# Memory layer of a decoder step: where the low part of the next weights stands on VectorE around y_b

## The chip, the cores and the metric

The kernel runs on one core of a Trainium2 chip. The metric is the device time of one execution in microseconds (us); it is given as the median of several runs. The engines are TensorE (PE in the profile; PEld is its weight load), VectorE (DVE), ScalarE (ACT), GpSimd (POOL) and SyncE (SP), which here only issues DMAs.

## The reference

One inference step of a two-layer decoder trunk on 320 tokens: 256 tokens of a new sequence and 8 samples of 8 tokens, with a model width of 1024. Layer 0 mixes tokens with a gated MLP, layer 1 with an mLSTM matrix memory; each is followed by a gated MLP with a width-3 convolution. Everything is fp32. The part that matters here is the mixer of layer 1, the memory layer:

```python
def mlstm_mixer(x, ...):
    p = x @ w_in                       # q, k, v, o and two gates; 8 heads
    qk, new_buf = causal_dwconv(qk_pre, ...); qk = silu(qk)
    h, C, n, m = mlstm_chunkwise(q, k, v, ig, lf, C0, n0, m0)
    hn = (h - mu) * rsqrt(var + EPS) * gn_g
    y = (sigmoid(o_pre) * hn) @ w_out
    return y, new_buf, C, n, m
```

Per head the chunkwise memory computes `sc = q k^T` weighted by gates, `num = q C + sc v` with its denominator, and the new state `C = decay C + k^T v`.

## The kernel before

**Layout.** Activations lie transposed: 128 features on the partitions, 320 tokens (T) along the free axis. A weight matrix is cut into blocks of 128 outputs, each of 8 tiles of 128 x 128 (512 KB). fp32 products are made from two parts: `split` rounds a tensor to a high part (fp32r) and takes the rest as low part; a block of the memory layer is 8 tiles times (high x high, high x low) in one sweep and then 8 times low weights x high activations in a second sweep (`chunk` with `low_last`), 24 matmuls.

**Weights.** `take` hands out the next block. It first calls `prefetch` (L121), which keeps four raw blocks loaded ahead (`raw`, four buffers, DMAs on SP's queue, L127) and one block split ahead: the high part `wh` is a copy on ScalarE (L154), the low part `wl` a subtraction on VectorE (L155). `wh` and `wl` have three buffers each. A raw buffer is free for the next load when both parts are made.

**Order.** A scheduler places the instructions of each engine by their dependencies; only TensorE's matmuls and a few others keep the order of the program. `tc.issue_after(ins)` adds an edge that puts the following instructions behind `ins` on the engine of `ins`.

**The loop over heads** (`layer_b`, the loop with `for h in range(NH)`; "pass h" below). Pass h, for h = 1 to 6, takes six blocks of head h: q, k, two of v, two of o. Between them it finishes the head before it:
- `qk_epi` (L755 on) scales a block of q or k (`bpad`), convolves it on VectorE (`bcv`), applies tanh on ScalarE (`bth`), and makes `qs` and the parts `qh`, `qhl`, `kh`, `khl`.
- `inter` and `numer` accumulate `num` of head h-1 on TensorE; `stats` makes mean and variance (`ns`, `dn`, `bstat`, `mv`, `rd`, `t`, and a power on GpSimd, `sl`), `normed` the normalised `hn` on ScalarE.
- `state_sample(h-1, i)`, i = 0 to 3, makes the new states of two samples each: two matmuls `pcs`, two VectorE updates of `C` (L1007), one store `out_Cs` on SP.
- `scores(h)` multiplies q and k (`psc`, with `kh` and `khl`), and makes the gate weights `w` on ScalarE from a row broadcast, `Mb`, that `rows_in(h)` loads from memory on SP (L794).
- `o_epi` (L1011) scales a block of o (`o_b`, VectorE) and takes its tanh on ScalarE (`th_o`).
- `finish(h-1)` (L1018) transposes `hn` on TensorE into two PSUM tiles `phn`, multiplies each by `1 + th_o` of head h-1 on VectorE (`y_b`, L1027), and splits the result into `yhb` (ScalarE, L1029) and `ylb` (VectorE, L1030).
- `k_nat` and `v_nat` transpose k and v of head h (`pk`, `pv`) and make `kgs`, `kgh`, `kgl`, `vh`, `vl` of them; `state_split` makes the parts `Ch`, `Cl` of the old states.

PSUM is in two pools: `psm` (3 buffers) for the blocks, `pk` and half of `pcs`, and `psa` (5 buffers) for `num`, `psc`, `phn`, `pv`, the state of the prompt (`pCp`) and the other `pcs`. The buffer of the first `phn` goes to the next head's `num`.

From the end of pass 4 on, blocks of the output projection (`early`, the table `EARLY_OUT`) come between: two after pass 4's k and v, one and two in each of passes 5 and 6. Pass 7 is written out separately.

In `finish` each half e makes its transposes, its `y_b` and its two parts before the next half begins. The `wl` of the second block after the o blocks is asked for by a `take` that comes later in the program, but it depends on nothing made in between, and in passes 1 to 6 the scheduler puts it ahead of the second `o_b`.

Of the kernel before, what the change touches and what calls it, by code (L numbers as in the profile page):

```python
# [10 lines left out]
F32 = mybir.dt.float32  # L11
# [3 lines left out]
MULT, ADD, SUB, MAX = ALU.mult, ALU.add, ALU.subtract, ALU.max  # L15

P = 128
# [3 lines left out]
T = TP + NB * NS  # L21
# [16 lines left out]
class Net:  # L38
# [597 lines left out]
    def layer_b(self):  # L636
        nc, tc, I, O = self.nc, self.tc, self.I, self.O
# [4 lines left out]
        with ExitStack() as ctx:  # L642
# [143 lines left out]
            def v_epi(h, j, ps):  # L786
                vT = lp.tile([P, 384], F32, tag="vT", name="vTb", bufs=2)
                nc.scalar.copy(vT[:, :T], ps[:, :T])
                nc.scalar.copy(vT[:, T:384], ps[:, TP:T])
                S[h].setdefault("vT", []).append(vT)  # L790

            def rows_in(h):
                mb = hp.tile([P, 392], F32, tag="Mb", name="Mb", bufs=2)
                nc.sync.dma_start(mb, I["rows"][h:h + 1, :].to_broadcast([P, 392]))  # L794
                S[h]["rows"] = mb
# [110 lines left out]
            def state_split(h, i):  # L906
                C0 = S[h]["C"][i]
                Ch = lp.tile([P, 2, CW], F32R, tag="Ch", name="Ch", bufs=3)
                Cl = lp.tile([P, 2, CW], F32R, tag="Cl", name="Cl", bufs=3)
                nc.scalar.copy(Ch, C0)  # L910
                low = nc.vector.tensor_tensor(Cl, C0, Ch.bitcast(F32), op=SUB)  # L911
                S[h].setdefault("Cs", []).append((Ch, Cl))
                return low

            def inter(h, i):

                s = S[h]
                if i == 0:
                    s["num2"] = self.psa.tile([P, 512], F32, tag="pa", name="num")
                d = s["num2"][:, :CW]  # L920
                Ch, Cl = s["Cs"][i]
                for u in range(2):
                    b = 2 * i + u
                    lhs = Qz[:, b * P:(b + 1) * P]
                    mm(d, lhs, Ch[:, u, :], b == 0, False)
                    mm(d, lhs, Cl[:, u, :], False, False)

            def numer(h):
                s = S[h]
                Ph, Pl, dec = s["P"]  # L930
                num = [self.psa.tile([P, 512], F32, tag="pa", name="num") for _ in range(2)] + [s["num2"]]
                d = num[2][:, :CW]
                mm(d, Ps, vh[:, 2, :], False, True)
                d = num[0][:, :CW]
                mm3(d, Ph[:, 0:P], Pl[:, 0:P], vh[:, 0, :], vl[:, 0, :], True, True)
                d = num[1][:, :CW]
                mm3(d, Ph[:, P:TP], Pl[:, P:TP], vh[:, 0, :], vl[:, 0, :], True, False)
                mm3(d, Ph[:, TP:384], Pl[:, TP:384], vh[:, 1, :], vl[:, 1, :], False, True)
                s["num"] = num
# [44 lines left out]
            def state_prompt(h):  # L984
                s = S[h]
                kgh, kgl, _, _ = s["kg"]
                pc = self.psa.tile([P, 512], F32, tag="pa", name="pCp")
                for t in range(2):
                    mm3(pc[:, :CW], kgh[:, t, :], kgl[:, t, :], vh[:, t, :], vl[:, t, :], t == 0, t == 1)

                Cp = hp.tile([P, CW], F32, tag="Cp", name="Cp", bufs=1)
                nc.scalar.copy(Cp, pc[:, :CW])
                nc.sync.dma_start(O["Cp"][h], Cp)

            def state_sample(h, i):
                s = S[h]
                kgz, dec, C0 = s["kg"][3], s["P"][2], s["C"][i]

                wide = h < NH - 2
                pcs = [pool.tile([P, 512], F32, tag=tag, name="pcs") for pool, tag in  # L1000
                       ((self.psa, "pa"), (self.psm, "pm") if wide else (self.psa, "pa"))]
                for u in range(2):
                    b = 2 * i + u
                    mm(pcs[u][:, :CW], kgz[:, b, :], vh[:, 2, :] if b < 4 else vb, True, True)
                for u in range(2):
                    b = 2 * i + u
                    made = nc.vector.scalar_tensor_tensor(C0[:, u, :], C0[:, u, :], dec[:, b:b + 1], pcs[u][:, :CW], op0=MULT, op1=ADD)  # L1007
                nc.sync.dma_start(O["Cs"][h, :, 2 * i:2 * i + 2, :], C0)
                return made
# [5 lines left out]
                nc.scalar.activation(th, o, AF.Tanh, scale=0.5)  # L1015
                S[h].setdefault("o", []).append(th)

            def finish(h):  # L1018
                s = S[h]
                yh = hp.tile([P, 2, T], F32R, tag="yhb", name="yhb", bufs=6)  # L1020
                yl = hp.tile([P, 2, T], F32R, tag="ylb", name="ylb", bufs=6)
                for e in range(2):
                    pt = self.psa.tile([P, 512], F32, tag="pa", name="phn")
                    for t in range(3):
                        self.tr(pt[:, t * P:(t + 1) * P], hn[:, t, e * P:(e + 1) * P], self.ident)
                    y = self.tp.tile([P, T], F32, tag="yf", name="y_b", bufs=2)
                    nc.vector.scalar_tensor_tensor(y, s["o"][e], 1.0, pt[:, :T], op0=ADD, op1=MULT)  # L1027
                    g = gnh[:, 2 * h + e:2 * h + e + 1]
                    nc.scalar.activation(yh[:, e, :], y, AF.Copy, scale=g)  # L1029
                    nc.vector.scalar_tensor_tensor(yl[:, e, :], y, g, yh[:, e, :].bitcast(F32), op0=MULT, op1=SUB)  # L1030
                    Y[2 * h + e] = (yh[:, e, :], yl[:, e, :])

            def early(h, r):
                for m in self.EARLY_OUT.get((h, r), ()):
                    self.residual(m, self.block(8, lambda k: Y[k]))
# [25 lines left out]
            def blk():  # L1061
                return self.block(KD, self.x_rhs)
# [19 lines left out]
            for h in range(NH):  # L1082
                if h:
                    rows_in(h)
                    qk_epi(h, 0, blk())
                    early(h, 0)
                    if h == 1:
                        inter(0, 0)
                        state_split(0, 3)
                    inter(h - 1, 1)  # L1090
                    qk_epi(h, 1, blk())
                    for i in (2, 3):
                        inter(h - 1, i)
                    numer(h - 1)
                    early(h, 1)
                    ps = blk()
                    with self.behind_split():
                        stats(h - 1)
                    v_epi(h, 0, ps)
                    state_prompt(h - 1)  # L1100
                    made = state_sample(h - 1, 0)
                    early(h, 2)
                    v_epi(h, 1, blk())
                last = h == NH - 1
                if last:
                    with tc.issue_after(made.ins):
                        made = normed(h - 1)
                    states(h, made)
                if h:
                    made = state_sample(h - 1, 1)  # L1110
                    if not last:
                        with tc.issue_after(made.ins):
                            normed(h - 1)
                scores(h)
                early(h, 3)
                if h and not last:
                    o_epi(h, 0, blk())
                if last:
                    finish(h - 1)
                    begin(0)  # L1120
                if h:
                    for i in (2, 3) if last else (2,):
                        state_sample(h - 1, i)
                if last:
                    begin(1)

                    self.prefetch(0, self.used + 2)
                early(h, 4)
                if h and not last:
                    states(h, made)  # L1130
                if h and not last:
                    o_epi(h, 1, blk())
                if h and not last:
                    finish(h - 1)
                    state_sample(h - 1, 3)
                k_nat(h)
                v_nat(h)
                if h:
                    inter(h, 0)
                    for i in (2, 3):  # L1140
                        low = state_split(h, i)
                else:
                    with tc.issue_after(self.parts[0].ins), tc.issue_after(self.parts[1].ins):
                        state_split(0, 2)
                early(h, 5)
            nc.sync.dma_start(O["b_state"], nst)

            h = NH - 1
# [181 lines left out]
```

## Time and profile before

| | |
|---|---|
| median of 3 runs | 953.72 us (953.01 to 955.09) |
| the profiled execution | 954.62 us |
| its span, first to last instruction | 952.9 us |
| granted TensorE clock, mean | 0.999 |
| instructions | 17084 |
| read from and written to HBM | 143.05 MB and 11.99 MB, 163 GB/s over the span |
| `wl` on VectorE (L155), 256 of them | 298.8 us, 1.168 us each |
| `wh` on ScalarE (L154), 256 of them | 256.7 us, 1.004 us each |

The profile is of one execution. A page gives busy times by engine and a chain of waits, followed back from the last instruction; further views give groups by line and tile, the waits, busy time by stretch, and a timeline. In a timeline a row is: start (us from the span's start), duration (us), engine, line, operation, out<-in, sizes, count, and in brackets how long the engine had been idle before and what ended that. Rows of SP are DMA issues, not the transfers. Matmuls overlap: a row shows some 0.31 us for one of 320 columns, and the next starts 0.15 us after it.

### The profile page before, as it was taken

To read this page: it belongs to the slowest core of one execution; us is meant where nothing else is said; L and a number is where in the kernel's file an instruction comes from. 1 tells how busy PE (TensorE), PEld (TensorE's weight loads), DVE (VectorE), ACT (ScalarE), POOL (GpSimd) and SP (SyncE) were. 2 spreads that over 40 slices of the span, in tenths; PEclk is the share of its full clock that TensorE was granted. 3 is DMA by queue.
4 is the path that set the end of the run, shared out by engine and by line. 5 is a ranking of instruction groups with operands and counts; after the bars stand their busy time and mean duration, and the time that the engine had idled before them with its cause. 6 is when DMAs were issued, how large, how long until landed. Compare 5 with 4: busy or idle time off the path is not lost.

```text
span 952.9 us, 17084 instructions
## 1 busy us (share of the span) xinstructions
PE 945.6 (99%) x6420; PEld 932.8 (98%) x6420; DVE 695.6 (73%) x1324; ACT 530.5 (56%) x978; POOL 117.6 (12%) x291
## 2 busy tenths in 40 slices
PE   9999999999999999999999999999999999999997
PEld 8889999999999999999999999999999999999997
DVE  6766976577777764559999998788888777775443
ACT  7557543454554443348877767666765544554342
POOL 3200000010000000014442312303001000000000
PEclk9999999999999999999999999999999999999999
DMA  8643346544444455565465756654474444445541
GB/s 272 209 153 133 130 134 190 175 140 150 153 156 147 141 159 156 146 215 176 155 201 185 219 174 207 198 183 133 132 250 144 156 148 145 151 150 152 145 138 56
DMA packets 55238, 156.15 MB, mean 164 GB/s; under 512 B 7492, under 2 KB 13132, under 8 KB 55156
## 3 DMA queue, kind: packets, MB, share of 16 engines
q1 hardware_dynamic: 55156, 155.06, 51.2%
q8 instruction: 51, 0.84, 0.3%
q14 instruction: 31, 0.25, 0.1%
HBM read 143.05 MB, written 11.99 MB: 163 GB/s over the span
## 4 chain that ended last, share of the span: by engine, by line
PE 93%; DVE 3%; ACT 1%; issue 1%; POOL 0%; DMA 0%; SPq 0%; POOLq 0%; ACTq 0%
PE pm L54 80%; PE pv_a L54 6%; PE num L54 2%; PE pmix L54 1%; PE pcs L54 1%; PE pCp L54 1%; PE phn L57 0%; PE psc L54 0%; DVE wl L155 0%; PE pv L57 0%; PE pc L54 0%; ACT wh L154 0%; PE pg L54 0%; DVE Cl L911 0%; DMA raw<-in_a_wv 0%
## 5 line engine op out<-in xcount | busy, mean ns | idle before, releaser
L154 ACT CAST wh<-raw 128x1024 fp32r<-128x1024 f32 (+3 forms) x256 | 256.7, 1004 | 270.8 <-PE pm L54 141.5
L155 DVE TENSOR_TENSOR wl<-raw,wh 128x1024 fp32r<-128x1024 f32 (+3 forms) x256 | 298.8, 1168 | 121.0 <-ACT wh L154 116.5
L54 PE MATMUL pm<-xh,wh 128*128 128x320 f32 x1216 | 372.2, 311 | 0.0
L54 PE MATMUL pm<-xl,wh 128*128 128x320 f32 x1216 | 370.3, 309 | 0.0
L54 PE MATMUL pm<-xh,wl 128*128 128x320 f32 x1216 | 321.2, 309 | 0.0
L54 PEld LDWEIGHTS pm<-xl,wh 128*128 128x128 f32 x1216 | 228.4, 188 | 0.2
L54 PEld LDWEIGHTS pm<-xh,wh 128*128 128x128 f32 x1216 | 228.3, 188 | 0.2
L54 PEld LDWEIGHTS pm<-xh,wl 128*128 128x128 f32 x1216 | 214.5, 188 | 0.0
L54 PE MATMUL pm<-yh_f,wh 128*128 128x320 f32 x352 | 108.8, 309 | 0.0
L54 PE MATMUL pm<-yl_f,wh 128*128 128x320 f32 x352 | 108.8, 309 | 0.0
L54 PE MATMUL pm<-yh_f,wl 128*128 128x320 f32 x352 | 108.8, 309 | 0.0
L54 PEld LDWEIGHTS pm<-yh_f,wh 128*128 128x128 f32 x352 | 66.1, 188 | 0.0
L54 PEld LDWEIGHTS pm<-yl_f,wh 128*128 128x128 f32 x352 | 66.1, 188 | 0.0
L54 PEld LDWEIGHTS pm<-yh_f,wl 128*128 128x128 f32 x352 | 66.1, 188 | 0.0
L532 DVE SCALAR_TENSOR_TENSOR fcv<-fpad,vecs,fcv 128x336 f32<-128x336 f32 x88 | 49.5, 565 | 2.1 <-ACT fcv L530 0.6
L54 PE MATMUL pm<-yh_a,wh 128*128 128x320 f32 x128 | 39.6, 310 | 0.0
L54 PE MATMUL pm<-yh_a,wl 128*128 128x320 f32 x128 | 39.5, 309 | 0.0
L54 PE MATMUL pm<-yl_a,wh 128*128 128x320 f32 x128 | 39.5, 309 | 0.0
L534 ACT ACTIVATE fgl<-fcv 128x256 f32<-128x256 f32 x44 | 18.3, 415 | 37.9 <-DVE fcv L532 37.8
L54 PE MATMUL pm<-yhb,wh 128*128 128x320 f32 x128 | 38.2, 311 | 0.0
L54 PE MATMUL pm<-ylb,wh 128*128 128x320 f32 x128 | 37.9, 309 | 0.0
L304 DVE TENSOR_TENSOR xT<-pm,xT 128x320 f32<-128x320 f32 x39 | 19.0, 488 | 24.7 <-PE pm L54 24.5
(289 smaller groups left out, 1366.5 us busy)
## 6 DMA issues: line engine op xcount, KB each, us to landing
raw<-in_f_up SPq DMA_DIRECT2D x88, 512.0 KB, 3.3
raw<-in_b_win SPq DMA_DIRECT2D x48, 512.0 KB, 4.1
raw<-in_f_dn SPq DMA_DIRECT2D x32, 448.0 KB, 3.4
C<-in_C SPq DMA_DIRECT2D x32, 258.0 KB, 3.9
out_Cs<-C SPq DMA_DIRECT2D x32, 258.0 KB, 4.0
raw<-in_a_win SPq DMA_DIRECT2D x16, 512.0 KB, 3.2
raw<-in_a_wo SPq DMA_DIRECT2D x16, 512.0 KB, 4.0
raw<-in_f_dn SPq DMA_DIRECT2D x16, 512.0 KB, 3.6
```

The costliest lines, as they stand in the source:

```text
L54: self.pin(self.nc.tensor.matmul(out, lhsT, rhs, start=start, stop=stop, skip_group_check=skip))
L154: self.last_split = self.hold(nc.scalar.copy(wh[:, :kn, :], raw[:, :kn, :]))
L155: self.last_low = nc.vector.tensor_tensor(wl[:, :kn, :], raw[:, :kn, :], wh[:, :kn, :].bitcast(F32), op=SUB)
L304: self.nc.vector.tensor_tensor(x, ps[:, :T], x, op=ADD)
L532: nc.vector.scalar_tensor_tensor(cv, pd[:, i:i + NC], self.vec(w + i * KF), cv, op0=MULT, op1=ADD)
L534: nc.scalar.activation(gl[:, :TP], cv[:, :TP], AF.Gelu_apprx_tanh)
```

## The change

`finish` gets an argument. Both halves now make their transposes and their `y_b` first. In passes 1 to 6 the argument is true: then `prefetch` is called behind the second `y_b`, with the number of blocks to be split raised by one, so that one more block is split there and the next `take` finds it done; its `wl` has to stand behind the second `y_b` on VectorE. Then both halves make their two parts. The calls of `finish` in pass 7 and after the loop keep their order of work apart from both `y_b` standing before the parts.

```diff
-            def finish(h):
+            def finish(h, ahead=False):
                 s = S[h]
                 yh = hp.tile([P, 2, T], F32R, tag="yhb", name="yhb", bufs=6)
                 yl = hp.tile([P, 2, T], F32R, tag="ylb", name="ylb", bufs=6)
+                ys = []
                 for e in range(2):
                     pt = self.psa.tile([P, 512], F32, tag="pa", name="phn")
                     for t in range(3):
                         self.tr(pt[:, t * P:(t + 1) * P], hn[:, t, e * P:(e + 1) * P], self.ident)
-                    y = self.tp.tile([P, T], F32, tag="yf", name="y_b", bufs=2)
-                    nc.vector.scalar_tensor_tensor(y, s["o"][e], 1.0, pt[:, :T], op0=ADD, op1=MULT)
+                    ys.append(self.tp.tile([P, T], F32, tag="yf", name="y_b", bufs=2))
+                    made = nc.vector.scalar_tensor_tensor(ys[e], s["o"][e], 1.0, pt[:, :T], op0=ADD, op1=MULT)
+                if ahead:
+                    with tc.issue_after(made.ins):
+                        self.prefetch(0, self.used + 2)
+                for e, y in enumerate(ys):
                     g = gnh[:, 2 * h + e:2 * h + e + 1]
                     nc.scalar.activation(yh[:, e, :], y, AF.Copy, scale=g)
                     nc.vector.scalar_tensor_tensor(yl[:, e, :], y, g, yh[:, e, :].bitcast(F32), op0=MULT, op1=SUB)
...
-                    finish(h - 1)
+                    finish(h - 1, True)
```

## The prediction

> **What bounds the kernel now.** I read the page's busy times first, then busy time by stretch, then the waits of TensorE's weight loads.
>
> ```profile
> PE 945.6 (99%) x6420; PEld 932.8 (98%) x6420; DVE 695.6 (73%) x1324; ACT 530.5 (56%) x978; POOL 117.6 (12%) x291
> PE 93%; DVE 3%; ACT 1%; issue 1%; POOL 0%; DMA 0%; SPq 0%; POOLq 0%; ACTq 0%
> ```
> ```profile
> 450.00:480.00 30.00, 29.60 (x213) 29.14 (x212) 28.87 (x73) 25.56 (x65) 12.80 (x22) 1.00 0.48 157
> ```
> ```profile
> 480.00:720.00 240.00, 239.96 (x1723) 239.65 (x1722) 209.27 (x479) 165.94 (x364) 51.37 (x79) 1.00 0.59 186
> ```
> ```profile
> PEld num L54 <- DVE y_b L1027: 0.5, 1, 0.5
> ```
>
> The columns of a stretch are its length and the busy time of PE, PEld, DVE, ACT and POOL. TensorE bounds the kernel: it is 99% busy and carries 93% of the chain, at full granted clock. In the rest of the memory layer (480 to 720 us) it is idle for 0.04 us, so nothing on VectorE can save time there. From 450 to 480 us it is idle for 0.40 us, and VectorE works 28.87 of 30 us. The one wait on VectorE in this layer that is worth naming is that on y_b: once, 0.5 us. This is pass 1 of the loop over heads:
>
> ```profile
> 475.94 1.21 DVE L155 TENSOR_TENSOR wl<-raw,wh 128x1024 fp32r<-128x1024 f32 x1
> ```
> ```profile
> 476.92 0.82 PE L57 MATMUL pv<-ident,vTb 128*128 128x128 f32 x6
> 477.07 0.47 DVE L1013 TENSOR_TENSOR o_b<-pm,rb 128x320 f32<-128x320 f32 x1
> ```
> ```profile
> 477.47 0.87 DVE L1027 SCALAR_TENSOR_TENSOR y_b<-th_o,phn 128x320 f32<-128x320 f32 x2
> ```
> ```profile
> 477.99 0.39 PE L54 MATMUL num<-Ch,Qz 128*128 128x258 f32 x1 [0.26 <-DVE y_b L1027]
> ```
>
> The accumulator `num` takes the PSUM buffer that the first y_b empties, so y_b behind wl makes TensorE wait. The chain of waits, one pass later, has the same six transposes and `num` right behind them without a wait (columns: start, us, what):
>
> ```profile
> 505.93 0.66 PE pv L57 x6
> 506.58 0.47 PE num L54 x4
> ```
>
> So in pass 1 `num` could have started at 476.92 + 0.66 = 477.58; it started at 477.99.
>
> **The change, part by part.**
>
> *Removed at pass 1.* Without wl ahead, o_b starts at 475.94, the first y_b at 476.34 and is done by about 476.8, well ahead of 477.58. The gain is 0.41 us; its bounds are 0.26 (PE's own idle time in the last row) and the 0.50 of PEld. wl itself then runs from 477.13 to 478.26. It belongs to the second block ahead, which starts at 482.73 (next fence) and uses its low part last, so its own delay is covered by 4 us.
>
> ```profile
> 482.73 3.52 PE pm L54 x24
> ```
> ```profile
> 488.40 3.52 PE pm L54 x24
> ```
> ```profile
> 563.75 10.56 PE pm L54 x72
> ```
>
> *The same move in passes 2 to 6.* No wait on y_b is there to take away. wl was filler while VectorE waited for the block of o:
>
> ```profile
> 503.00 1.21 DVE L155 TENSOR_TENSOR wl<-raw,wh 128x1024 fp32r<-128x1024 f32 x1
> 504.81 0.49 DVE L1013 TENSOR_TENSOR o_b<-pm,rb 128x320 f32<-128x320 f32 x1 [0.60 <-PE phn L57]
> ```
>
> Now that gap stays partly empty and wl stands in front of y's low parts, the last state update (C), kgs, vl and the next head's work: all of it comes up to 1.13 us (475.94 to 477.07) later. No instruction and no transfer is added: there are as many wl, wh and raw loads as before. But the schedule follows. In the changed program's instruction order three things differ in passes 2 to 4:
> 1. On VectorE `ns` and a statistic stand ahead of q's and k's `qs`, and wl of the o block stands ahead of k's `qs`.
> 2. On ScalarE `ns`, `vh` and two `dn` stand ahead of `bth` (they were behind it).
> 3. On SP the order before the load of the next rows (Mb) was: out_Cs, raw, C, out_Cs, Mb. It is now: out_Cs, C, raw, out_Cs, Mb. raw waits for the moved wl, the second out_Cs for the moved C, and Mb queues behind both.
>
> The step that can hold TensorE is the last one, through Mb. In pass 3:
>
> ```profile
> 505.23 0.38 SPq L127 DMA_DIRECT2D raw<-in_b_win  x1
> 508.00 0.33 SPq L903 DMA_DIRECT2D C<-in_C  x1
> 508.42 0.39 SPq L1008 DMA_DIRECT2D out_Cs<-C  x1
> 508.86 0.42 SPq L794 DMA_DIRECT2D Mb<-rows  x1
> ```
> ```profile
> 514.42 1.04 ACT L811 ACTIVATE w<-Mb,cols 128x256 f32<-128x256 f32 x3 [1.53 <-DMA Mb<-rows]
> 515.37 1.04 ACT L154 CAST wh<-raw 128x1024 fp32r<-128x1024 f32 x1
> 516.31 1.14 ACT L910 CAST Ch<-C 128x516 fp32r<-128x516 f32 x2
> 517.35 0.49 ACT L772 ACTIVATE bth<-bcv 128x344 f32<-128x344 f32 x1
> 517.75 0.66 ACT L768 ACTIVATE bcv<-bpad,vecs 128x344 f32<-128x344 f32 x1
> 518.43 0.37 ACT L945 COPY ns<-num 64x258 f32<-64x258 f32 x1
> 518.83 0.41 ACT L861 CAST vh<-vh 32x256 fp32r<-32x256 f32 x1
> ```
> ```profile
> 506.41 1.18 DVE L1030 SCALAR_TENSOR_TENSOR ylb<-y_b,gnh,yhb 128x320 fp32r<-128x320 f32 x2
> ```
> ```profile
> 507.50 0.48 DVE L1007 SCALAR_TENSOR_TENSOR C<-C,Mb,pcs 128x258 f32<-128x258 f32 x1
> ```
> ```profile
> 522.96 0.26 DVE L312 TENSOR_TENSOR khl<-qs,kh 128x128 fp32r<-128x128 f32 x1
> ```
> ```profile
> 525.04 0.28 PE L54 MATMUL psc<-qh,khl 128*128 128x256 f32 x1
> ```
>
> ScalarE waits for Mb already now, with everything behind it, and TensorE needs khl at 525.04, 1.8 us after it is made. The working; on VectorE the next instruction starts 0.08 us ahead of the end that a row shows (wl: 1.21 shown, 1.13 to the next start), so each takes that much less than its row:
> - PE is 0.41 us early, so o_b starts at 504.40; o_b and both y_b take 1.18, wl 1.13, y's low parts 1.10, the two C 0.80: C is done at 508.6 (now 507.98). out_Cs follows at once, Mb 0.44 later: 509.05. It landed 5.56 us after issue here (508.86 to 514.42). So w starts at 514.6.
> - bth now stands behind w, wh, Ch (2.93 us), ns, vh (0.83) and two dn (0.2): it starts at w + 3.96 and ends at w + 4.4. Behind it on VectorE come qs, the three bcv of k (waiting for ScalarE's bcv, w + 5.1), qhl, the statistics, wl and k's qs, together 4.8 us, then C and khl, 0.6: khl ends at w + 10.3 = 524.9 to 525.0.
> - TensorE, 0.41 early, wants it at 524.63. It waits about 0.35 us.
>
> In pass 4 the same sum gives:
>
> ```profile
> 538.34 0.42 SPq L794 DMA_DIRECT2D Mb<-rows  x1
> ```
> ```profile
> 542.79 1.04 ACT L811 ACTIVATE w<-Mb,cols 128x256 f32<-128x256 f32 x3 [1.56 <-DMA Mb<-rows]
> ```
> ```profile
> 553.40 0.28 PE L54 MATMUL psc<-qh,khl 128*128 128x256 f32 x1
> ```
>
> From khl to the second o_b VectorE has 8.25 us of work (two wl, four C, three Cl, Pf, Pl, Ps, the first o_b and small ones, at the pitches of this trace), so it gets there at about 533.2; C is done at 537.4, Mb goes out at 538.4 behind C and raw and lands after 4.45 us: w at 542.85, khl at 553.15, needed at 553.40 less the 0.06 us still gained. No wait, but 0.2 us of slack. In pass 2 w runs ahead of all this:
>
> ```profile
> 474.76 0.51 ACT L811 ACTIVATE w<-Mb,cols 128x256 f32<-128x256 f32 x1
> ```
> ```profile
> 496.70 0.28 PE L54 MATMUL psc<-qh,khl 128*128 128x256 f32 x1
> ```
>
> There the chain starts where `numer` ends, at 488.40 - 0.41: ns, vh, dn and bth end at 489.45, khl 5.9 later at 495.35, wanted at 496.29: 0.9 us of slack. From the end of pass 4 on three output blocks give TensorE 10.56 us more work per pass (72 matmuls, as long as the 72 at 563.75, which are two of them and the next q) and VectorE idles ahead of o_b, which holds the moved 1.13 us:
>
> ```profile
> 600.40 0.49 DVE L1013 TENSOR_TENSOR o_b<-pm,rb 128x320 f32<-128x320 f32 x1 [1.42 <-PE phn L57]
> ```
>
> y's low parts are first used by TensorE in pass 4, 13 matmuls of 0.147 us into the first output block: 565.65. They end at 564.9 with wl ahead. That is covered by 0.7 us.
>
> *Sum.* -0.41 + 0.35 = -0.06 us, against a profiled execution of 954.62 us (span 952.9 and 1.7 around it): 954.6. It ran 0.90 us above the median of the runs, 953.72; on that footing the forecast is **953.7 us**: what pass 1 gains, pass 3 takes back. The unknown is Mb's landing. All seven:
>
> ```profile
> DMA to landing us min/median/max: 4.3/4.7/5.5
> ```
>
> At 4.3 w starts at 513.4 and khl is in time: the sum is -0.41. Above 5.5 there is no row; the price with one more raw load ahead is the rival below. I take 5.56, the row of that very pass.
>
> **Rivals.**
> 1. *The gain stays.* Mb lands within 5.2 us, or ScalarE is not held, and nothing later waits: -0.41, that is 953.3 us (bounds -0.26 and -0.50). For it: the median landing is 4.7. Against it: in pass 3 it was 5.5, with less in front of it.
> 2. *Slower: Mb behind raw.* raw is now issued behind the C load, just ahead of the second out_Cs and of Mb, instead of 3.6 us ahead (505.23 against 508.86). If Mb has to wait for all of raw, the price is raw's own transfer, 512 KB at the rate of a full stretch:
>
> ```profile
> 507.00:508.00 1.00, 1.00 (x9) 1.00 (x8) 0.95 (x2) 1.00 (x4) 0.00 (x0) 1.00 1.01 382
> ```
>
> The last column is GB/s: 524,288 bytes at 382 GB/s are 1.37 us. khl in pass 3 is then 0.35 + 1.37 = 1.72 us late. TensorE comes out 1.3 us behind, VectorE starts pass 4's end at 534.5 and Mb goes out at 539.25, landing at 545.1; khl at 555.4 against 554.7: 0.7 us more. -0.41 + 1.72 + 0.7 = +2.0, that is **955.7 us**. It decides from w later than 514.8 in pass 3 (net zero). For it: raw, C, out_Cs and Mb all go out on SP's queue (the rows above), and the DMA share, the last column but one, is full there (1.01). Against it: in pass 4 the 516 KB of C and out_Cs just ahead of Mb did not keep it from landing in 4.45 us. The Trainium skill, "DMA: Bandwidth & Descriptors", section "Queues, rings and completion order", speaks for this rival: on each engine descriptors are consumed in ring order, and a transfer's signal lands only after the earlier writes of that engine. No row of this trace has raw directly ahead of Mb.
> 3. *Another wait that I have not priced*, on one of the PSUM buffers that passes 2 to 4 hand on differently: within 1 us either way per pass, up to 2 us.
>
> That the change does not do what it says is excluded by the instruction order: wl stands behind both y_b in passes 1 to 6.
>
> **How the numbers follow.** Given back (953.7, own range 953.2 to 954.4): 0.47. The gain stays (953.3): 0.25. Mb behind raw (955.7): 0.18. Unpriced wait: 0.10. A measurement of this kernel can tell about 0.2%, 1.9 us, from no change: above 955.6 or below 951.8. The first two cases lie within it. Of the third a little over half lies above, 0.10; of the fourth 0.03 on either side. So: faster 0.03, same 0.84, slower 0.13. The range takes in the first two and most of the third, with the shown runs' scatter of 0.7 us below the median: 952.7 to 955.8.
>
> **What would show it.** Right: no wait on y_b in pass 1, `num` some 0.4 us earlier against the end of pv; w of pass 3 at 514 to 515 and a wait of the psc matmul (or of the block of o behind it) for khl, C or kh of 0.1 to 0.7 us; blocks at the same pace everywhere else. Rival 1: PE idle under 0.1 us from 450 to 720. Rival 2: Mb landing after 6.5 us or more, and waits at psc in passes 3 and 4. Wrong altogether: a wait of TensorE in passes 5 to 7, for a weights' part, or a change outside the memory layer.

## The result and the profile after

| | before | after |
|---|---|---|
| median | 953.82 us (953.01 to 955.94, 15 runs) | 957.06 us (955.09 to 958.92, 15 runs) |
| the profiled execution, and its span | 954.62 us, 952.9 us | 956.65 us, 954.9 us |

The ratio is 1.003, 95% interval 1.0023 to 1.0038: slower by 2.9 us (2.2 to 3.6), above the forecast of 953.7 and outside its range, which ended at 955.8. Two stretches of the changed kernel's busy times (length, then PE, PEld, DVE, ACT and POOL, then granted clock, DMA share and GB/s):

```profile
450.00:480.00 30.00, 29.87 (x217) 29.65 (x216) 28.57 (x73) 25.56 (x63) 11.54 (x22) 1.00 0.47 159
480.00:720.00 240.00, 238.45 (x1698) 237.76 (x1697) 210.90 (x478) 162.75 (x361) 52.51 (x79) 0.99 0.58 186
```

Up to 480 us TensorE is idle for 0.13 us where it was 0.40: the wait on y_b is gone. Behind 480 us it is idle for 1.55 us where it was 0.04, and the clock's mean is no longer 1.00. The waits of the weight loads name the place (us in total, times, longest):

```profile
PEld psc L54 <- ACT kh L312: 1.7, 1, 1.7
PEld psc L54 <- DVE khl L312: 0.5, 2, 0.2
```

And the chain of waits tells what stands behind it and what comes after it (start, us, what):

```profile
509.29 6.36 DMA Mb<-rows
...
518.73 0.38 ACT ns L945
519.12 0.41 ACT vh L861
...
519.78 0.39 ACT bth L772
...
523.75 1.13 DVE wl L155
...
525.60 0.50 PE psc L54 x2
...
526.91 5.10 PE pm L54 x24
```

Read it from the bottom. The block behind psc takes 5.10 us; each block of 24 matmuls took 3.52 before. Ahead of it psc waited for kh, which waited for k's qs behind a wl, for bth behind ns and vh, and all of these for Mb, which landed 6.36 us after its issue. That is pass 3, the place that the prediction named, with a far larger wait. ScalarE's timeline from there (start, us, in brackets the idle time before):

```profile
515.68 0.51 ACT L811 ACTIVATE w<-Mb,cols 128x256 f32<-128x256 f32 x1 [2.50 <-DMA Mb<-rows]
516.09 1.04 ACT L154 CAST wh<-raw 128x1024 fp32r<-128x1024 f32 x1
...
517.57 1.13 ACT L910 CAST Ch<-C 128x516 fp32r<-128x516 f32 x2
...
519.67 0.49 ACT L772 ACTIVATE bth<-bcv 128x344 f32<-128x344 f32 x1
...
525.25 0.30 ACT L312 CAST kh<-qs 128x128 fp32r<-128x128 f32 x1 [1.18 <-DVE qs L774]
```

w starts at 515.68, forecast 514.6. From w to the end of khl (525.80 + 0.28) it is 10.4 us, forecast 10.3; before, it was 8.8 (514.42 to 523.22). The length of that chain was forecast well, its start was not. SP's queue shows why the start moved (rows are issues, not transfers; first the changed kernel, then the row of before that stands ahead of those shown in the prediction):

```profile
502.91 0.37 SPq L127 DMA_DIRECT2D raw<-in_b_win  x1
503.38 0.38 SPq L1008 DMA_DIRECT2D out_Cs<-C  x1
507.96 0.33 SPq L903 DMA_DIRECT2D C<-in_C  x1
508.38 0.38 SPq L127 DMA_DIRECT2D raw<-in_b_win  x1
508.86 0.38 SPq L1008 DMA_DIRECT2D out_Cs<-C  x1
509.29 0.42 SPq L794 DMA_DIRECT2D Mb<-rows  x1
```
```profile
504.75 0.38 SPq L1008 DMA_DIRECT2D out_Cs<-C  x1
```

The C load overwrites the buffer that the store out_Cs just ahead of it reads, so SP stands there until that store has landed: 4.58 us in the changed kernel (503.38 to 507.96), 3.25 before (504.75 to 508.00). Everything behind it in the queue stands with it: the second raw, the next out_Cs (its C was done at 507.21 + 0.88 = 508.09) and Mb. The prediction had out_Cs "at once" behind C and Mb 0.44 later; Mb went out 1.20 us after C. The raw just ahead of this store is new there: it is the load that stood ahead of the store before this one in the old order (at 498.05). That it makes the store land later is what e9 and e10 test.

The slow block has a cause of its own. Three stretches of the changed kernel, cut where the granted clock changes (the last column but two):

```profile
524.11:527.52 3.41, 1.89 (x12) 1.68 (x13) 3.41 (x11) 2.08 (x6) 2.25 (x2) 1.00 0.51 137
527.52:530.94 3.42, 3.42 (x15) 3.42 (x14) 3.39 (x10) 2.23 (x6) 0.00 (x0) 0.50 0.94 237
530.94:534.35 3.41, 3.41 (x25) 3.41 (x25) 3.33 (x7) 1.63 (x3) 0.00 (x0) 1.00 0.58 206
```

In the first TensorE was idle for 1.5 us, in the second its clock is at half: 15 matmuls where the third has 25. The block lost 5.10 - 3.52 = 1.58 us.

Idle time shows less than TensorE loses, since a matmul's row ends later than the next one can start. The starts of the same six transposes, `pv`, at the ends of passes 1, 2, 3 and 4 show the whole. The kernel before, behind the row at 476.92 us in the prediction, then the changed kernel:

```profile
505.76 0.82 PE L57 MATMUL pv<-ident,vTb 128*128 128x128 f32 x6
534.10 0.82 PE L57 MATMUL pv<-ident,vTb 128*128 128x128 f32 x6
```
```profile
476.57 0.82 PE L57 MATMUL pv<-ident,vTb 128*128 128x128 f32 x6
504.91 0.82 PE L57 MATMUL pv<-ident,vTb 128*128 128x128 f32 x6
536.83 0.82 PE L57 MATMUL pv<-ident,vTb 128*128 128x128 f32 x6
```

From pass 1 to pass 2 TensorE takes 28.34 us where it took 28.84: a gain of 0.50. From pass 2 to pass 3 it takes 31.92 where it took 28.34: a loss of 3.58, of which the wait for kh is 1.49, a shorter one for khl some 0.3 and the slow block 1.58. From pass 3 to pass 4 it loses 0.29 more (28.65 to the pv at 565.48, against 28.36 to the one at 562.46). Together that is 3.4 us. The spans differ by only 2.0, because in these two executions the changed kernel was 0.35 us ahead at the first of these rows already and 1.0 us shorter behind 675 us.

### The profile page after: what moved, and what is told of

It is laid out like the page before. It is cut to its first block, busy times and chain, and to the rows that moved or that the text cites. A ratio compares the mean times of both kernels' runs of the same rounds, so it can differ in the third digit from the quotient of the medians.

```text
span 954.9 us, 17086 instructions
## 1 busy us (share of the span) xinstructions
PE 947.2 (99%) x6420; PEld 934.4 (98%) x6420; DVE 699.2 (73%) x1324; ACT 529.3 (55%) x978; POOL 121.7 (13%) x291
## 4 chain that ended last, share of the span: by engine, by line
PE 94%; DVE 3%; ACT 1%; issue 1%; DMA 1%; POOL 0%; SPq 0%; POOLq 0%; ACTq 0%
PE pm L54 80%; PE pv_a L54 6%; PE num L54 2%; PE pmix L54 1%; PE pcs L54 1%; DMA Mb<-rows 1%; PE psc L54 1%; PE pCp L54 1%; PE phn L57 0%; PE pv L57 0%; DVE wl L155 0%; PE pc L54 0%; PE pw L54 0%; ACT wh L154 0%; PE pg L54 0%
## 5 line engine op out<-in xcount | busy, mean ns | idle before, releaser
L523 DVE TENSOR_TENSOR fpad<-pm,rb 128x256 f32<-128x256 f32 x44 | 18.7, 425 | 24.9 <-PE pm L54 24.2
```

The source lines that it names most:

```text
L523: nc.vector.tensor_tensor(pd[:, 2:258], ps[:, :TP], self.rb[:, :TP], op=MULT)
```

## The experiments

Theory A: Mb of pass 3 lands too late, because of what the moved wl does to SP's queue; the wait and the half-speed block are all of the loss. Rival B: wl in front of VectorE's work costs a share in each pass. Within A it was open whether the raw ahead of Mb counts (A1), the late C (A2), or the order on ScalarE and VectorE with it (A3).

The forecasts are absolute times. The runs of the kernel before that were taken along had a median of 954.08 us for e1 to e4, 954.34 for e5 to e8 and 953.95 for e9 to e12, and each ratio is against those. "From pv to pv" is TensorE's time between the transposes named above, compared with the kernel before.

**e1: the move in pass 1 alone.**

```diff
-                    finish(h - 1, True)
+                    finish(h - 1, h == 1)
```

> The moved wl in pass 1 alone; passes 2 to 6 as before. Theory A (the loss is one wait of TensorE in pass 3, for kh and khl, because Mb lands late behind the raw that the wl moved in pass 2 holds up, and half-speed matmuls behind that wait): the wait on y_b goes and nothing comes back, 0.4 us less than before, 953.4 us; no wait at psc, granted clock 1.00 from 480 to 720 us. Theory B (wl in front of VectorE's later work costs wherever it is done): about one sixth of the loss, 954 us.

954.56 us (953.48 to 955.89, 11 runs), ratio 1.0005 (0.9996 to 1.0014). TensorE is idle for 0.15 us from 450 to 480 us and for 0.18 us from 480 to 720, with no wait at psc: as A has it, that wait and the slow block are gone. The forecast of 0.4 us less is missed. From pv to pv TensorE gains 0.50 us up to pass 2 and loses 0.29 up to pass 3 and 0.43 up to pass 4, where num waits for a y_b again, behind the wl of passes 2 and 3. The time alone does not tell A from B here, since a sixth of the loss lies inside the interval.

**e2: in all passes but pass 2** (`h != 2`).

> The move in passes 1, 3, 4, 5 and 6, not in pass 2. Theory A: pass 3 is as before, with Mb landing after 4 to 5.6 us; the gain of 0.4 us stays and pass 4 costs 0 to 0.3 us: 953.4 to 953.8 us. Theory B (the loss is spread over the passes): most of it stays, 956 us or more, with a wait at psc in a pass other than 3.

955.4 us (953.83 to 958.04, 11 runs), ratio 1.0017 (1.0008 to 1.0026). Neither forecast held. The profiled execution, the shortest of the eleven at 953.83 us, shows no wait (TensorE idle 0.04 us from 480 to 720, Mb landing within 5.0), but the others were longer by up to 4.2 us, and none of those was profiled. So the wait that pass 2's move brings is not all: a part of the loss stays in most runs, and where it falls is not shown.

**e3: a third buffer for Mb in the changed kernel.**

```diff
-                mb = hp.tile([P, 392], F32, tag="Mb", name="Mb", bufs=2)
+                mb = hp.tile([P, 392], F32, tag="Mb", name="Mb", bufs=3)
```

> The changed kernel with a third buffer for Mb and nothing else: VectorE's and TensorE's order stay as they are, each Mb is issued one pass earlier, and w stands earlier on ScalarE. Theory A: no wait at psc in pass 3, no half-speed block, 953.3 to 953.6 us. Theory B (it is the order on VectorE, ns and wl ahead of k's qs, that holds khl): the wait at psc stays at over 1 us and the time at 956.5 to 957.5 us.

954.25 us (953.37 to 954.95, 11 runs), ratio 1.0001 (0.9992 to 1.001). VectorE's order is that of the changed kernel to the last instruction, and the loss is gone, though the gain of pass 1 (0.50 us from pv to pv) does not show in the time:

```profile
480.00:720.00 240.00, 240.00 (x1724) 239.94 (x1724) 213.13 (x482) 165.68 (x365) 48.60 (x79) 1.00 0.61 188
```

That ends rival B: what VectorE does later costs nothing, as long as w does not wait for Mb.

**e4: the changed kernel again**, for a second profile.

> The changed kernel once more, unchanged, for a second profile. Theory A: Mb of pass 3 lands 6 us or more after its issue again and psc waits 1.2 us or more. If the landing after 6.4 us was chance, it lands within 5.6 us and psc waits under 0.5 us; the time of this look is then below 955 us.

957.88 us. Mb of pass 3 landed 6.3 us after its issue and psc waited again, and a second wait came in pass 4:

```profile
525.95 0.39 PE L54 MATMUL psc<-qh,kh 128*128 128x256 f32 x1 [1.51 <-ACT kh L312]
```
```profile
555.99 0.38 PE L54 MATMUL psc<-qh,kh 128*128 128x256 f32 x1 [1.11 <-ACT kh L312]
```

The clock stayed at 1.00 here. From pv to pv the two executions of one kernel lose nearly the same between passes 1 and 4, 3.4 and 3.3 us, in two ways: 1.5 us and a half-speed block (which makes TensorE so late that pass 4 has time to spare), or 1.5 and 1.1 us. Pass 4's queue on SP:

```profile
534.71 0.37 SPq L127 DMA_DIRECT2D raw<-in_b_win  x1
535.18 0.38 SPq L1008 DMA_DIRECT2D out_Cs<-C  x1
539.99 0.33 SPq L903 DMA_DIRECT2D C<-in_C  x1
540.41 0.38 SPq L127 DMA_DIRECT2D raw<-in_b_win  x1
540.88 0.38 SPq L1008 DMA_DIRECT2D out_Cs<-C  x1
541.32 0.42 SPq L794 DMA_DIRECT2D Mb<-rows  x1
```

Its C was done at 538.8 (537.97 + 0.87). SP stood at the C load until 539.99, and Mb went out 2.5 us behind C instead of the 1.0 forecast (C done at 537.4, Mb at 538.4). The kernel before had this already: in its pass 4 C was done at 536.32, the C load on SP went out at 537.47, and Mb 2.0 us behind C.

**e5: the second raw behind Mb.** One swap on SP; all else in the order of the changed kernel. (In e5, e9, e10 and e11 the lines of the rows are higher by 2 to 12.)

```diff
+        if self.raws == 2 and self.rows_made is not None:
+            with self.tc.issue_after(self.rows_made.ins):
+                yield
```

> The changed kernel with one swap on SP: each second raw of a pass is issued behind Mb instead of ahead of it; VectorE's and ScalarE's order stay. Theory A1 (Mb is late because raw's 512 KB stand right ahead of it): Mb of pass 3 is issued 0.4 us earlier and lands 5.0 to 5.5 us after its issue, at least 1.3 us earlier in all; the waits at psc shrink from 1.5 to at most 0.4 us, no half-speed block, 953.5 to 954.5 us. Theory A2 (Mb is late because C and out_Cs are, and raw does not matter): the landing comes 0.4 us earlier and no more, psc waits about 1.1 us, 956 us or more.

956.43 us (954.9 to 958.94, 11 runs), ratio 1.0022 (1.0013 to 1.0031): the time forecast is missed. The landing came near to what A1 says, 5.6 us, and psc in pass 3 waits 0.3 us. But pass 4 waits 1.1 us, and the time hardly gains (a further 0.3 us is a wait for a `wl` at 700 us):

```profile
554.70 0.39 PE L54 MATMUL psc<-qh,kh 128*128 128x256 f32 x1 [1.12 <-ACT kh L324]
```

In pass 4 the C load went out 4.85 us behind the store (534.04 to 538.89), and Mb at 539.74, 2.2 us behind C. Raw ahead of Mb is one cause, not the cause.

**e6: bth ahead of ns on ScalarE**, by holding the statistics behind q's tanh. This gives back the order of before on ScalarE, and with it k's qs ahead of the wl on VectorE; some raw loads on SP move with it.

```diff
-                    with self.behind_split():
+                    with self.behind_split(), tc.issue_after(S[h]["th", 0].ins):
```

> The changed kernel with the statistics of the head before held behind q's bth on ScalarE, which gives back the order of before there (bth ahead of ns, vh and dn) and on VectorE (k's qs ahead of a wl and of rd). Mb stays behind raw and as late as in the changed kernel. Theory A3 (the loss needs both: Mb late by 1.3 to 1.9 us, and 1.0 us on ScalarE and 1.1 us on VectorE put in front of kh, against 1.85 us that kh had to spare before): kh of pass 3 comes at about w + 7.9 us, psc waits 0 to 0.3 us, 953.5 to 954.5 us. If Mb's landing alone holds TensorE: the wait at psc stays at 1.2 us or more and the time at 956.5 us or more.

954.92 us (953.62 to 956.84, 11 runs), ratio 1.0009 (1.0 to 1.0018): most of the loss is gone, though the time is above the forecast. Pass 3 does not test A3 in this execution, since Mb landed 5.45 us after its issue and not 6.4: measured from the pv ahead of it, w was 0.7 us later than before (2.1 in the changed kernel). Pass 4 does. By the same measure w was 1.9 us late there, as in e4 (1.7) and e5 (1.7), where psc waits 1.1 us. ScalarE in pass 4:

```profile
544.38 0.51 ACT L811 ACTIVATE w<-Mb,cols 128x256 f32<-128x256 f32 x1 [2.34 <-DMA Mb<-rows]
...
552.53 0.30 ACT L312 CAST kh<-qs 128x128 fp32r<-128x128 f32 x1 [0.24 <-DVE qs L774]
```

From w to kh it takes 8.2 us here, 9.6 in e4 (546.06 to 555.63) and 8.1 before (542.79 to 550.89), and psc does not wait. A new wait of 0.3 us on vh in pass 4 is what the moved statistics cost (0.80 from pv to pv). So A3 holds, by pass 4: the loss needs both, a late Mb and 1.5 us more behind it.

**e7: the move in pass 2 alone** (`h == 2`).

> The move in pass 2 alone, the other passes as before. Theory A: the wait on y_b in pass 1 stays (0.3 to 0.5 us), the wait at psc in pass 3 comes with 1.2 to 1.5 us (TensorE is not 0.4 us early), then either half-speed matmuls (1.6 us) or nothing: 955.2 to 957 us. Theory B (every pass adds a share): 954.5 us.

956.02 us (954.8 to 958.31, 11 runs), ratio 1.0022 (1.0013 to 1.0031). psc waits 1.2 us in pass 3, y_b's wait in pass 1 stays. No raw stands ahead of the store of pass 3 here: the C load goes out 3.2 us behind it and Mb 0.88 us behind C, both as before. But the second raw stands ahead of Mb, which lands 6.4 us after its issue. So that wait does not need the late store. By the times e7 and e2 cannot be told apart (1.0022 and 1.0017), so which pass's move carries more is not shown.

**e9: the first raw behind the store.** Only the raw that stands ahead of the first out_Cs in the rows above goes behind it.

```diff
+        if self.raws == 1 and self.store is not None:
+            with self.tc.issue_after(self.store.ins):
+                yield
```

> The changed kernel with the first raw of each pass issued behind the store out_Cs of pair 2 instead of ahead of it; everything else on SP, VectorE and ScalarE keeps its order (the second raw still stands ahead of Mb). Theory S (SP stands at the C load until that store has landed, 4.6 to 4.9 us when raw goes out ahead of it and 3.3 to 3.4 us when not, and the second raw, out_Cs and Mb queue behind): C of passes 3 and 4 goes out 3.2 to 3.6 us after the store; Mb of pass 4 goes out about 1 us nearer to the end of its C (538.1 to 538.6 us plus what TensorE has lost by then); the wait at psc in pass 4 goes (0 to 0.3 us) and that of pass 3 shrinks to 0.5 to 1.0 us; 954.2 to 955.6 us. If the store lands as late without raw ahead of it: both waits stay, 956.5 to 957.5 us.

956.45 us (956.01 to 959.54, 6 runs), ratio 1.0028 (1.0016 to 1.0039). The store lands earlier, as theory S says: the C load goes out 3.0 us after it in pass 3 and 3.5 in pass 4, and psc in pass 3 does not wait at all. Pass 4 does, for 0.96 us:

```profile
533.91 0.38 SPq L1020 DMA_DIRECT2D out_Cs<-C  x1
...
537.39 0.33 SPq L915 DMA_DIRECT2D C<-in_C  x1
537.82 0.38 SPq L129 DMA_DIRECT2D raw<-in_b_win  x1
538.29 0.38 SPq L1020 DMA_DIRECT2D out_Cs<-C  x1
538.73 0.42 SPq L806 DMA_DIRECT2D Mb<-rows  x1
```

Mb is issued early, with the second raw right ahead, and lands after 5.75 us (w at 544.48). The forecast of the waits was the wrong way round, and the time is higher than this one wait explains: from pv to pv TensorE loses 0.26 and 1.54 us less the 0.51 of pass 1, 1.3 in all, the clock is at 1.00 there, and the ratio stands for 2.7 us. What the rest is these runs do not show.

**e10: both swaps, e5's and e9's.** ScalarE and VectorE keep the order of the changed kernel.

> Both swaps on SP in the changed kernel: the first raw behind the store of pair 2, the second behind Mb; VectorE and ScalarE keep the order of the changed kernel. Theory S with A1: Mb goes out right behind C's store in both passes and lands within 5.2 us; psc waits 0 to 0.4 us in pass 3 and 0 to 0.2 us in pass 4, 953.4 to 954.4 us. If the order on VectorE and ScalarE alone holds kh: waits of 1 us or more stay, 956 us or more.

954.49 us (953.23 to 955.56, 11 runs), ratio 1.0001 (0.9993 to 1.001).

```profile
480.00:720.00 240.00, 240.00 (x1725) 239.93 (x1724) 213.54 (x483) 164.69 (x365) 52.48 (x81) 1.00 0.60 188
```
```profile
532.13 0.38 SPq L1020 DMA_DIRECT2D out_Cs<-C  x1
532.60 0.38 SPq L129 DMA_DIRECT2D raw<-in_b_win  x1
535.59 0.33 SPq L915 DMA_DIRECT2D C<-in_C  x1
536.74 0.34 SPq L1020 DMA_DIRECT2D out_Cs<-C  x1
537.13 0.42 SPq L806 DMA_DIRECT2D Mb<-rows  x1
```

No wait at psc is left and the loss is gone, by the place of two raw loads on SP alone. Each alone left a wait in pass 4. The numbers side by side, in us and from timeline rows, each for pass 3 and pass 4 (the last column: from pv of pass 2 to that of pass 3, and on to that of pass 4). From Mb's issue to w is the landing where w waits for Mb; in pass 3 of e10 it does not.

| kernel | store to C load | C to Mb | Mb to w | waits at psc for kh | from pv to pv, against before |
|---|---|---|---|---|---|
| before | 3.25, 3.43 | 0.88, 2.02 | 5.56, 4.45 | none | |
| after | 4.58, 4.55 | 1.20, 1.41 | 6.39, 4.42 | 1.5, 0 (half-speed block) | 3.58, 0.29 |
| after again (e4) | 4.74, 4.81 | 1.29, 2.48 | 6.31, 4.74 | 1.5, 1.1 | 2.08, 1.69 |
| e5 | 4.60, 4.85 | 0.85, 2.20 | 5.58, 5.04 | 0.3, 1.1 | 0.90, 1.70 |
| e6 | 4.08, 4.57 | 0.74, 2.98 | 5.45, 4.43 | none | 0, 0.80 |
| e9 | 3.00, 3.48 | 0.42, 1.33 | 5.36, 5.75 | 0, 0.96 | 0.26, 1.54 |
| e10 | 2.72, 3.46 | 0.42, 0.42 | 4.75, 5.10 | none | 0, 0.02 |

**e11: both swaps and bth first.**

> Both swaps on SP, and bth ahead of ns on ScalarE: what is left of the change is wl behind y_b in six passes. Theory A3 with S: no wait at psc, at vh or at y_b above 0.1 us, granted clock 1.00, 953.3 to 954.0 us. If wl behind y_b has a price of its own that neither explains: 954.8 us or more.

954.01 us (952.84 to 954.5, 11 runs), ratio 0.9998 (0.9989 to 1.0007); TensorE idle for 0.15 us from 450 to 480 and 0.00 from 480 to 720. Wl behind y_b has no price of its own that these runs can tell. Nor is there a version that beats the kernel before by more than the interval: e3, e10 and e11 keep the 0.50 us that TensorE gains in pass 1 from pv to pv, but the intervals reach 0.9 us either way.

**e8 and e12: waits made on purpose**, in the kernel before, to see what drops the clock. The copies write qs onto itself.

```diff
+                for _ in range({2: 13, 3: 13, 4: 15, 5: 11, 6: 21}.get(h, 0) * j):
+                    nc.scalar.copy(qs[:, :P], qs[:, :P])
```

> The kernel before with copies of qs onto itself ahead of kh on ScalarE (13, 13, 15, 11 and 21 of them in passes 2 to 6), so that TensorE waits at psc for about 0.3, 0.8, 1.2, 1.6 and 2.0 us. Theory G (an idle stretch of TensorE of 1 us or more can drop its granted clock to half for one stretch of 3.4 us): one or more half-speed stretches of 3.4 us follow the longer waits and none the short ones; each costs 1.6 us beyond its wait. Theory H (the half-speed stretch of the first profile had nothing to do with the wait): the clock stays at 1.00 from 440 to 720 us and the time is that of before plus the waits.

976.39 us. The copies took 0.33 us each, so the waits came longer than planned: 2.8, 2.1, 2.7, 2.1 and 6.4 us. Half speed followed the third and the fifth. Two pairs of stretches, the second wait without it and the third with it:

```profile
529.00:532.42 3.42, 1.77 (x13) 1.74 (x14) 3.40 (x8) 2.90 (x10) 0.00 (x0) 1.00 0.77 181
532.42:535.83 3.41, 3.41 (x25) 3.41 (x24) 2.06 (x7) 2.13 (x5) 0.00 (x0) 1.00 0.75 271
559.72:563.14 3.42, 1.07 (x8) 1.04 (x9) 3.41 (x8) 3.26 (x12) 0.00 (x0) 1.00 0.87 249
563.14:566.55 3.41, 3.41 (x15) 3.41 (x15) 1.69 (x5) 0.94 (x3) 0.00 (x0) 0.50 0.52 205
```

> The kernel before with 9, 11, 12, 9 and 8 copies of qs onto itself ahead of kh in passes 2 to 6, which by the pitch of the run before (0.33 us each) give idle stretches of TensorE of 1.5, 1.5, 1.7, 1.4 and 2.1 us. Theory G2 (the clock drops for a stretch of 3.41 us on a fixed grid when TensorE was idle for more than about 1.5 us of the stretch before): half speed follows only where 1.5 us or more of the idle time lies in one stretch of the grid. If it hangs on the length of the wait alone: it follows all of 1.5 us and more, or none.

964.66 us, with waits of 1.5, 1.5, 1.7, 1.5 and 1.1 us and none followed by half speed. The largest idle time within one stretch of the grid (described at the end) was 1.46 us, so G2's threshold was not crossed: the run does not contradict G2, and it does not prove it. In e8 1.54 and 1.65 us had left the clock at full speed, so a threshold of 1.5 is too low for those.

## Why the prediction was wrong

- *The wait on y_b in pass 1 goes.* Right. From pv to pv TensorE gains 0.50 us, the upper of the two bounds, where 0.41 was forecast; its idle time fell by 0.27 only (0.40 to 0.13).
- *No instruction is added, and wl behind y_b is covered.* Right: e3, e10 and e11 do all of it at no cost.
- *The chain from Mb through ScalarE and VectorE to khl in pass 3.* Right in place and length: 10.4 us, forecast 10.3.
- **The step that failed is "out_Cs follows at once, Mb 0.44 later ... it landed 5.56 us after issue here", and for pass 4 "Mb goes out at 538.4 behind C and raw and lands after 4.45".** Mb's issue was counted from VectorE's C alone. SP's queue stands at the C load until a store has landed, which the raw now ahead of that store had made 1.3 us longer, and two more issues stand between. The prediction's list of SP's order begins at that store, so this raw is not in it; and that the queue stands there could be seen before, in pass 4's 2.02 us from C to Mb. Against the second o_b, Mb of pass 3 went out 0.68 us later than forecast (509.29 - 503.96 = 5.33 against 509.05 - 504.40 = 4.65) and landed 0.83 later (6.39 against 5.56): 1.5 us, which turns the forecast wait of 0.35 into the 1.8 that psc's khl matmul was late (1.49 for kh and 0.30 for khl). In pass 4 it was 1.4 later in e4 (541.32 - 534.70 = 6.62 against 538.4 - 533.2 = 5.2), and Mb landed 0.3 later (4.74 against 4.45); that eats the 0.2 us of slack and gives the 1.1 us for kh and some 0.3 for khl. Added up from pv to pv, the change is -0.50 + 3.58 + 0.29 us in the changed kernel's profile, where -0.41 + 0.35 was forecast.
- *Not priced at all: the half-speed block*, 1.58 us when it comes.
- *Rival 2, "Mb behind raw", +2.0 us, chance 0.18*, was the nearest. By the trace's records of DMA packets (Mb's are those of 1,568 bytes) the first packet of Mb in pass 3 started 1.76 us after its issue before, 2.99 in the changed kernel and 1.79 in e5: 1.2 us for a raw right ahead (only a store's issue stands between), priced at 1.37. In passes 3 and 4 of all profiles it was 2.8 to 3.1 us with a raw issued 0.9 us ahead of Mb and 1.1 to 2.0 without. It had been given the smaller chance on one row of pass 4 (4.45 us behind C and out_Cs), in which no raw stood right ahead of Mb. The rule of the Trainium skill that was named with it, from "DMA: Bandwidth & Descriptors", section "Queues, rings and completion order", agrees with e5 in so far as raw's place decides when Mb's packets start; that a store behind raw also lands later (4.6 to 4.9 us in the changed kernel, e4 and e5, against 2.7 to 3.5 in e9 and e10) was the second half that the rival lacked.
- *The range* ended at 955.8 because rival 2's two terms were summed without a wait of full size in pass 4 and without the clock. *Passes 5 and 6* cost nothing, as forecast.

## What to carry to other kernels

When a step moves, follow each queue in order: in these traces a DMA on SP went out not when its data were ready but when every issue ahead of it had been let go, so each load ahead of it that waits for a store's landing has to be in the sum. A transfer that no wait shows today may have less than 2 us to spare; look how long the instruction that needs it stands ready, and price the case that the queue in front of it changes. Where a wait of 1.5 us or more is possible on TensorE, name the half-speed stretch that may follow as a risk, with its price of 1.6 us. And measure a gain by the starts of the same instruction in both kernels, not by idle time alone.

## What the runs showed of the hardware

The granted clock changes on a grid: in the changed kernel and in e8 all full-speed stretches between changes are whole multiples of 3.413 us (522.24, 423.25, 556.37 and 78.51 us are 153, 124, 163 and 23 of them), and a drop between two of them lasts one or two. Idle time within one stretch of the grid and the clock of the next: in e8 and e12 1.29, 1.34, 1.46, 1.54 and 1.65 us left it at full speed and 2.35, 2.40 and 3.41 us were followed by half speed, and 1.52 us in the changed kernel were too. So idle time decides by the stretch and not by the wait (a wait of 2.8 us in e8, cut in two by the grid, did nothing, nor did e4's of 1.51, of which 1.30 lay in one stretch), but between 1.5 and 1.7 us these runs do not tell what decides. The Trainium skill, "TensorE: Matmul & The Clock Gate", Part 1, has the same window of about 3.4 us, free-running, but lets the clock drop after at least one idle window; here windows that were idle for 1.52 and 2.35 of their 3.41 us were enough.

By the trace's records of DMA packets nine tenths of Mb's 128 packets had ended at 513.42 us in pass 3 of the changed kernel, and the last eight one after the other up to 515.15, as if one of the DMA engines had been held up. The DMA share (last column but one) shows this tail:

```profile
513.00:514.00 1.00, 1.00 (x9) 1.00 (x9) 1.00 (x2) 0.17 (x1) 0.00 (x0) 1.00 0.25 94
514.00:515.00 1.00, 1.00 (x11) 1.00 (x10) 1.00 (x2) 0.00 (x0) 0.00 (x0) 1.00 0.06 24
```

In the other profiles the tail of pass 3 was 0.5 to 1.7 us long, and 0.2 in e8, e10 and e11; it was 1.1 before. In pass 4 of the changed kernel the first packet came as late as in pass 3 (3.08 us after the issue, 1.99 before), but the tail was 0.2 us long and w started 4.42 us after the issue, as before (4.45). So a raw right ahead delays Mb's first packet and not always its landing. What makes the tail was not tried, and so how much of the 6.39 us is owed to raw and how much to the tail stays open.
